# Output projection of a hybrid encoder layer: eight plain quarter products against the seven products of one Strassen step

## The chip, the cores and the metric

One core of one Trainium2 chip runs the kernel. The metric is the device time of one execution in microseconds (us). Four compute engines work side by side, each through its own queue in order: TensorE (PE: matrix products into the PSUM memory; PEld is its weight load), VectorE (DVE), ScalarE (ACT) and GpSimd (POOL). SyncE (SP) issues the DMA transfers. Instructions wait for each other through semaphores; an instruction that waits holds up all that stands behind it in its engine's queue.

## The reference, cut to what is changed

```python
y = jnp.concatenate([y_pool, y_attn], axis=-1)          # (1, 1024, 1024) f32
y = jnp.einsum('bsm,md->bsd', y, w_out[l])              # output projection, 1024 x 1024 x 1024
h = h + gate[:, None, :] * y                            # gate comes from the conditioning vector c
```

`y_pool` (512 channels) comes from pooling and a gate, `y_attn` (512 channels) from eight attention heads and a gate. Everything ahead of these lines is the same in both kernels.

## The kernel before, in words

All activations lie with channels on the 128 partitions and the 1024 positions along a row. The gated input of the projection is eight tiles of 128x1024: `yp[0..3]` (pool) and `gT[0..3]` (attention; `gT[i]` is complete when heads 2i and 2i+1 are). Precision is kept by splitting every float32 operand in two: `hi`, a copy rounded to the type that TensorE multiplies, and `lo`, the rest. A product is then three matmuls: hi by hi, hi by lo, lo by hi.

Attention is software pipelined over 64 jobs (8 heads, 8 jobs each; the loop at L1005). In one step, TensorE makes scores of one job and weighted sums of an older one (`attend`, L842), ScalarE the exponentials (L819) and their hi part (L824, `p_hi`), GpSimd the lo part (L831, `p_lo`; two of eight jobs on VectorE). When a half head is done, `out_copy` (L864) takes the sums out of PSUM: a ScalarE copy (L868) and a VectorE add (L869), both into `rb`. The next half head writes the same PSUM tile, so its `attend` waits for L869. Then VectorE takes a reciprocal (L875), GpSimd normalises (L879, `op`), TensorE turns the tile (L887, `yt`), VectorE brings it into `gT`.

`extra` (L946 and below) hangs further work into steps of that loop, by hand: `out_split` cuts two weight tiles of the projection into hi (ScalarE) and lo (GpSimd, L937), `y_split` (L900) cuts the finished tiles of y (hi on ScalarE or VectorE, L914 and L916; lo on VectorE, L918), and `fill` (L969) begins output tile 0 between the last attention matmuls.

The projection has eight output tiles. For each, `fill` issues 8 (channel tiles) x 3 (hi/lo) x 2 (halves of the positions) matmuls of 128x512 into two PSUM banks (L974, the last tile in the loop at L1110 with two of its pieces 256 wide), 384 matmuls of 512 columns by their sum. Then `out_end` (L977) adds the gated sum to x on VectorE and SP writes it out. After the attention loop GpSimd has nothing to do; VectorE makes the eight columns of the gate (`mod_col`, L108, eight instructions of 128x1024), and for each output tile one lo of 128x1024 and two final adds of 128x512.

Of the kernel before, what the change touches and what calls it, by code (L numbers as in the profile page):

```python
# [32 lines left out]
XH = 6  # L33
XS = (4, 5)
XS2 = (2, 2)
YP = ((0, 4, 5, 1), (1, 6, 7, 1), (2, 8, 8, 1), (3, 9, 9, 0), (4, 10, 10, 0), (5, 11, 11, 0), (6, 12, 12, 0))
NF = 7
SG = 12
LAG = 6
LPARTS = ((0, 512), (512, 768), (768, 1024))  # L40
# [11 lines left out]
RT = ("xh4", "xl4", "xh5", "xh1")  # L52
# [6 lines left out]
def body(ctx, tc, small, cond, xT, ada_sc, ada_sh, ada_gt, w_lat, w_fm, pool_w, w_uq, w_ukv, gains, pos, w_out, out):  # L59
# [837 lines left out]
    yh, yl = [None] * NK, [None] * NK  # L897
    yq, yk = [], []

    def y_split(k, halves=(0, 1), parts=(0, 1), he=A):  # L900
        if not yq:
            yq.append(qp.tile([P, 6, S], F32R, tag="QT", name="yq"))
            yk.append(qp.tile([P, 6, S], F32R, tag="KT", name="yk"))
        if 0 in halves and 0 in parts and k < 6:
            t_, j = (yq, yk)[k // 3][0], 2 * (k % 3)
            yh[k], yl[k] = t_[:, j], t_[:, j + 1]
        elif 0 in halves and 0 in parts:
            pool, th, tl = ((xp, "xh0", "xl0"), (dp, "t1", "t2"))[k - 6]
            yh[k] = pool.tile([P, S], F32R, tag=th, name=f"yh{k}")
            yl[k] = pool.tile([P, S], F32R, tag=tl, name=f"yl{k}")  # L910
        y = (yp + gT)[k]
        c_ = slice(halves[0] * 512, halves[-1] * 512 + 512)
        if 0 in parts and he is A:
            A.activation(yh[k][:, c_], y[:, c_], AF.Copy)  # L914
        elif 0 in parts:
            he.tensor_copy(yh[k][:, c_], y[:, c_])  # L916
        if 1 in parts:
            V.tensor_tensor(yl[k][:, c_], y[:, c_], f32(yh[k][:, c_]), ALU.subtract)  # L918

    ow = {}  # L920

    def out_load(d):
        raw = wp.tile([P, NK, P], F32, tag="raw", name=f"oraw{d}")
        SY.dma_start(raw, w_out[d])
        ow[d] = [raw]

    def out_split(d, halves=(0, 1), parts=(0, 1), eng=V):
        if 0 in halves and 0 in parts:
            for m, tag in enumerate(("whi", "wlo")):
                ow[d].append(xp.tile([P, NK, P], F32R, tag=f"x{'hl'[m]}{d + 2}", name=f"o{tag}{d}") if d < 2 else  # L930
                             wp.tile([P, NK, P], F32R, tag=tag, name=f"o{tag}{d}"))
        raw, hi, lo = ow[d]
        c_ = slice(halves[0] * 4, halves[-1] * 4 + 4)
        if 0 in parts:
            A.activation(hi[:, c_], raw[:, c_], AF.Copy)  # L935
        if 1 in parts:
            eng.tensor_tensor(lo[:, c_], raw[:, c_], f32(hi[:, c_]), ALU.subtract)  # L937
# [12 lines left out]

    at(*OL, out_load, 0)
    at(OL[0], OL[1] + 1, out_load, 1)
    for n in range(2):
        for part in range(2):
            for d in range(2):
                at(XH + d, XS[part] + XS2[d] * n, out_split, d, (n,), (part,), G)

    xr, ps = {}, {}

    def res_load(d):  # L960
        xr[d] = xp.tile([P, S], F32, tag=RT[d % 4], name=f"xres{d}")
        SY.dma_start(xr[d], xT[d])

    def new(d):
        pool, tag = (stp, "st") if d % 3 < 2 else (rsp, "r")
        t_ = pool.tile([P, 2, 512], F32, tag=tag, name=f"ops{d}")
        ps[d] = [t_[:, 0], t_[:, 1]]

    def fill(d, k0, k1, ns=(0, 1)):  # L969
        hi, lo = ow[d][1:]  # L970
        for k in range(k0, k1):
            for j, (w_, y_) in enumerate(((hi, yh), (hi, yl), (lo, yh))):
                for n in ns:
                    T.matmul(ps[d][n], w_[:, k, :], y_[k][:, n * 512:(n + 1) * 512],  # L974
                             start=(k == 0 and j == 0), stop=(k == NK - 1 and j == 2))

    def out_end(d, n):  # L977
        c_ = slice(n * 512, n * 512 + 512)
        V.scalar_tensor_tensor(xr[d][:, c_], ps[d][n], gate[:, d:d + 1], xr[d][:, c_], ALU.mult, ALU.add)
        if n:  # L980
            SY.dma_start(out[d], xr[d])
# [10 lines left out]
    at(7, 8, new, 0)  # L992
    for k in range(NF):
        at(7, 8 + k, fill, 0, k, k + 1)
    for k, s0, s1, e_ in YP:
        at(7, s0, y_split, k, (0, 1), (0,), (A, V)[e_])
        at(7, s1, y_split, k, (0, 1), (1,))
# [75 lines left out]
    fill(0, NF, 7)  # L1073
    out_tr(H - 1, (0,), avp.tile([P, 2, 512], F32, tag="av", name="ytl"))
    V.scalar_tensor_tensor(gT[3], last[0], vinv, gT[3], ALU.mult, ALU.mult)
    y_split(7)
    for d in range(2):
        res_load(d)
    out_load(2)
    for d in range(4):  # L1080
        gate_cols(d)
    new(1)
    fill(1, 0, 4)
    fill(0, 7, 8)
    for d in range(NK):
        mod_col(gate[:, d:d + 1], gc.pop(d), cb2[0])
        if d + 4 < NK:
            gate_cols(d + 4)
        if d == 3:
            out_split(2)  # L1090
    V.tensor_tensor(gate, gate, adab_s[:, 16:24], ALU.add)
    fill(1, 4, 8)
    for d in range(2, NK):
        if d + 1 < NK:
            out_load(d + 1)
# [27 lines left out]
        if d + 1 < NK:  # L1123
            out_split(d + 1)
# [69 lines left out]
```

## Time and profile before

| | us |
|---|---|
| median of three timed runs | 501.43 (501.01 to 503.52) |
| the profiled execution, its own time | 500.05 |
| span of the profiled execution | 498.3 |
| last attention sums and turned tiles on TensorE | about 409 to 416.6 |
| last matmul ends, last VectorE add ends | 494.9, 495.45 |

After the last add stand 2.85 us to the end of the span (the output transfer), and 1.75 us more to the execution's own time. Rows of the timeline read: start, duration, engine, line, operation, output<-inputs, shapes, and in brackets idle time before it with what ended that. On VectorE a row's duration runs some 0.08 us into the next row's start, so the pitch of two rows that follow each other is the time that the engine is held.

### The profile page before, as it was taken

How to read it: one execution, taken by the hardware profiler on the slowest of the kernel's cores; microseconds unless marked ns; L12 is line 12 of the kernel's file. 1: busy time of each engine (PE TensorE's matmuls, PEld its weight loads, DVE VectorE, ACT ScalarE, POOL GpSimd, SP SyncE). 2: the span in 40 equal slices, each digit the busy share in tenths (PEclk: the TensorE clock that was granted, in tenths of full speed). 3: DMA queues.
4: the chain of work that ended last, by engine and by line, in shares of the span. 5: the costliest groups of instructions: out<-in, count | busy, mean ns of one | idle time of the engine just before them, and what ended most of it. 6: DMA issues, size and time to landing. Idle time of an engine off the chain costs nothing.

```text
span 498.3 us, 7657 instructions
## 1 busy us (share of the span) xinstructions
PE 464.9 (93%) x2956; PEld 355.0 (71%) x2956; DVE 355.9 (71%) x565; ACT 253.8 (51%) x338; POOL 234.4 (47%) x190
## 2 busy tenths in 40 slices
PE   5999998999999999999989888898898969999997
PEld 3999876898888888785555555555555658888886
DVE  4888849999999853577677887877867985913221
ACT  3756038993203030226878888888899861001000
POOL 1950040201242949448869796787869780000000
PEclk9999999999999999999999999999999999999999
DMA  8894442000102110144786779779982836753333
GB/s 300 332 307 159 171 142 65 6 1 7 47 1 91 34 58 27 57 86 95 170 148 138 162 145 176 152 151 163 224 175 63 160 113 231 276 182 129 126 128 126
DMA packets 117046, 66.33 MB, mean 133 GB/s; under 512 B 105873, under 2 KB 107793, under 8 KB 117010
## 3 DMA queue, kind: packets, MB, share of 16 engines
q1 hardware_dynamic: 117010, 65.85, 49.9%
q8 instruction: 23, 0.38, 0.3%
q14 instruction: 13, 0.11, 0.1%
HBM read 35.43 MB, written 4.19 MB: 80 GB/s over the span
## 4 chain that ended last, share of the span: by engine, by line
PE 49%; DVE 22%; ACT 10%; POOL 10%; issue 5%; DMA 3%; SPq 0%; ACTq 0%; DVEq 0%; POOLq 0%
PE ops L974 14%; PE fps L170 8%; PE st L800 4%; PE pq L548 3%; ACT ph L824 3%; PE lps L234 3%; DVE bp L808 3%; POOL fraw L152 3%; ACT p L819 3%; DMA wlr<-in_w_lat 2%; PE rs L730 2%; PE av L849 2%; PE st L804 2%; POOL s L614 2%; DVE ph L831 2%
## 5 line engine op out<-in xcount | busy, mean ns | idle before, releaser
L831 POOL TENSOR_TENSOR ph<-p,ph 128x1024 f16<-128x1024 f32 x49 | 105.9, 2168 | 13.1 <-ACT ph L824 10.2
L170 PE MATMUL fps<-xh,whi 128*128 128x512 f32 x192 | 62.0, 404 | 0.5 <-ACT whi L147 0.5
L170 PE MATMUL fps<-xh,wlo 128*128 128x512 f32 x192 | 59.3, 390 | 0.1
L170 PE MATMUL fps<-xl,whi 128*128 128x512 f32 x192 | 59.3, 390 | 0.0
L800 PE MATMUL st<-q,k 97*128 97x512 f16 x192 | 49.5, 379 | 6.7 <-ACT p L819 6.6
L804 PE MATMUL st<-k,q 97*128 97x512 f16 x192 | 48.2, 379 | 8.0 <-ACT p L819 6.4
L824 ACT ACTIVATE ph<-p 128x1024 f16<-128x1024 f32 x49 | 51.7, 1055 | 0.5
L152 POOL TENSOR_TENSOR fraw<-fraw,shift 128x1024 f32<-128x1024 f32 x7 | 22.7, 3237 | 60.8 <-DVE wlo L148 53.8
L808 DVE TENSOR_REDUCE bp<-st 128x1 f32<-128x1024 f32 x32 | 39.0, 1220 | 5.2 <-PE st L804 3.4
L170 PEld LDWEIGHTS fps<-xh,whi 128*128 128x128 f32 x192 | 35.5, 189 | 9.0 <-ACT whi L147 1.0
L170 PEld LDWEIGHTS fps<-xh,wlo 128*128 128x128 f32 x192 | 36.0, 188 | 8.1 <-DVE wlo L148 0.5
L170 PEld LDWEIGHTS fps<-xl,whi 128*128 128x128 f32 x192 | 36.1, 188 | 7.7
L935 ACT ACTIVATE owhi<-oraw 128x1024 fp32r<-128x1024 f32 (+1 forms) x10 | 8.8, 885 | 54.0 <-DMA oraw<-in_w_out 54.0
L819 ACT ACTIVATE p<-st,bp,esc 128x1024 f32<-128x1024 f32 x25 | 30.1, 1204 | 9.4 <-DVE bp L809 9.0
L804 PEld LDWEIGHTS <-q 97*128 97x128 f16 x192 | 16.6, 97 | 25.6 <-issue 10.9
L800 PEld LDWEIGHTS <-k 97*128 97x128 f16 x192 | 16.6, 97 | 21.5 <-issue 8.3
L624 ACT ACTIVATE dh<-s 128x1024 fp32r<-128x1024 f32 x4 | 4.2, 1062 | 51.9 <-DVE s L621 51.9
L819 ACT ACTIVATE p<-st,ebias,esc 128x1024 f32<-128x1024 f32 x24 | 28.9, 1203 | 2.5 <-PE st L800 1.3
L850 PE MATMUL av<-VT,ph 128*128 128x65 f16 x256 | 26.4, 193 | 2.9 <-POOL ph L831 2.9
L849 PE MATMUL av<-VT,pt 128*128 128x129 f16 x256 | 28.0, 221 | 0.8 <-DMA pt<-ph 0.8
L849 PE MATMUL av<-VT,ph 128*128 128x129 f16 x256 | 27.7, 221 | 0.2 <-DVE rb L869 0.2
L850 PEld LDWEIGHTS <-ph 128*128 128x128 f16 x256 | 22.6, 98 | 7.1 <-POOL ph L831 3.1
(297 smaller groups left out, 1142.5 us busy)
## 6 DMA issues: line engine op xcount, KB each, us to landing
fraw<-in_w_fm SPq DMA_DIRECT2D x12, 512.0 KB, 3.7
asc<-in_ada_sc SPq DMA_DIRECT2D x8, 512.0 KB, 6.0
xr<-in_xT SPq DMA_DIRECT2D x8, 512.0 KB, 5.3
ash<-in_ada_sh SPq DMA_DIRECT2D x8, 512.0 KB, 6.8
oraw<-in_w_out SPq DMA_DIRECT2D x8, 512.0 KB, 5.1
xres<-in_xT SPq DMA_DIRECT2D x8, 512.0 KB, 5.0
agt<-in_ada_gt SPq DMA_DIRECT2D x8, 512.0 KB, 5.7
out_dram<-xres SPq DMA_DIRECT2D x7, 512.0 KB, 3.0
```

Of the source, the lines that this page charges most:

```text
L152: G.tensor_tensor(pb, pb, shift.unsqueeze(2).broadcast_to([P, NK, P]), ALU.mult)
L170: T.matmul(ps[n], w[:, k, :], x_[k][:, n * 512:(n + 1) * 512], start=(k == order[0] and j == 0), stop=(k == order[-1] and j == 2))
L234: T.matmul(ps[:, :LAT], l[k][:, ts_], r[k], start=(k == 0 and i == 0), stop=(k == NK - 1 and i == 2))
L800: T.matmul(stt[i][:, n], l[:HW, kt * P:(kt + 1) * P], r[:HW, 0:512], start=(a == 0), stop=(a == 2))
L804: T.matmul(stt[i][:, n], l[:HW, qt * P:(qt + 1) * P], r[:HW, n * 512:(n + 1) * 512], start=(a == 0), stop=(a == 2))
L808: V.tensor_reduce(bps[i], stt[i], AX.XY, ALU.max)
L819: A.activation(pfs[i], st, AF.Exp, bias=bps.pop(i) if hf else ebias, scale=esc)
L824: A.activation(pas[i][:, 0], pfs[i], AF.Copy)
L831: (V if in_psum(i) else G).tensor_tensor(pas[i][:, 1], pfs[i], pas[i][:, 0], ALU.subtract)
L849: T.matmul(o_, hi, VT[:, kt, h, 0:129], start=kt == 0 and qt % 2 == 0, stop=False, skip_group_check=True)
L850: T.matmul(o_[:, 0:65], lo, VT[:, kt, h, 0:65], start=False, stop=kt == NK - 1, skip_group_check=True)
L974: T.matmul(ps[d][n], w_[:, k, :], y_[k][:, n * 512:(n + 1) * 512], start=(k == 0 and j == 0), stop=(k == NK - 1 and j == 2))
```

## The change

The projection is done as one step of Strassen's algorithm in Winograd's form. Weights, y and output are cut in quarters: output tiles 0-3 and 4-7, channel tiles 0-3 (pool) and 4-7 (attention), positions 0-511 (`H0`) and 512-1023 (`H1`). Eight products of quarters become seven, each 4 output tiles x 4 channel tiles x 3 matmuls of 128x512, so 12 matmuls for one product `prod(c, d)` of one output tile, 28 such products, 336 matmuls of 512 columns in all. `a11`, `a12`, `a22` are quarters of the weights, `s1` to `s4` sums and differences of them; `b11`, `b21`, `b22` are quarters of y, `t1` to `t4` sums and differences of them. All those sums are made in float32 before the split in hi and lo.

Who does what:

- sums of y (`t1`, `t23`, `t4_split`): one VectorE instruction of 128x512 each, 16 in all, all operands in SBUF; each of the seven y operands, four channel tiles each, is then split, hi on ScalarE (`b11` and half of `t1` on VectorE), lo on VectorE;
- sums of weights (`w_comb`): VectorE, 16 in all; each of the 28 weight tiles is split, hi on ScalarE, lo on GpSimd (128x512 each);
- partial results that are used twice (`keep`): copied out of PSUM by ScalarE, 12 of 128x512, and added to x by VectorE (`pre_add`), 12 of 128x512 with both inputs in SBUF;
- the last use of a PSUM bank (`final`): VectorE adds it to x, 16 of 128x512, and SP writes 128x512 at a time.

Work moved into the attention loop: `b11` in heads 6 and 7 (VectorE, 8 instructions of 128x512), `t1` in head 7, and behind it, among the last weighted sums, `a11` and `s1` products and their weights. The gate columns (`mod_col`) stand between the splits of `t3` and `b22`.

The diff, cut to its core:

```diff
-    def fill(d, k0, k1, ns=(0, 1)):
-        hi, lo = ow[d][1:]
-        for k in range(k0, k1):
-            for j, (w_, y_) in enumerate(((hi, yh), (hi, yl), (lo, yh))):
-                for n in ns:
-                    T.matmul(ps[d][n], w_[:, k, :], y_[k][:, n * 512:(n + 1) * 512],
-                             start=(k == 0 and j == 0), stop=(k == NK - 1 and j == 2))
...
+    def t1(k, part, he=V):
+        if part == 0:
+            V.tensor_tensor(yp[k][:, H1], yp[k][:, H1], yp[k][:, H0], ALU.subtract)
+            b_hi("t1", k, yp[k][:, H1], he)
+        else:
+            b_lo("t1", k, yp[k][:, H1])
+    def t23(k):
+        V.tensor_tensor(yp[k][:, H1], gT[k][:, H1], yp[k][:, H1], ALU.subtract)
+        V.tensor_tensor(yp[k][:, H0], yp[k][:, H1], yp[k][:, H0], ALU.subtract)
+    def split(c, k, src):
+        b_hi(c, k, src)
+        b_lo(c, k, src)
+    def t4_split(k):
+        in_ring("t4", k)
+        V.tensor_tensor(yp[k][:, H1], gT[k][:, H0], yp[k][:, H1], ALU.subtract)
+        split("t4", k, yp[k][:, H1])
...
+    def w_comb(c, d, parts=(0, 1), leng=G):
...
+            if c == "s1":
+                V.tensor_tensor(src, a2[:, F_], a2[:, L_], ALU.add)
+                V.tensor_tensor(a2[:, F_], a1[:, F_], a2[:, F_], ALU.subtract)
+            elif c == "s2":
+                V.tensor_tensor(src, a2[:, L_], a2[:, F_], ALU.subtract)
+            elif c == "s4":
+                V.tensor_tensor(src, a1[:, L_], a1[:, F_], ALU.subtract)
+            A.activation(hi, src, AF.Copy)
+        if 1 in parts:
+            leng.tensor_tensor(lo, src, f32(hi), ALU.subtract)
...
+    def prod(c, d, k0=0, k1=4, cols=slice(0, 512)):
...
+        for k in range(k0, k1):
+            for j, (w_, y_) in enumerate(((hi, B[b][0]), (hi, B[b][1]), (lo, B[b][0]))):
+                T.matmul(ps[d][n][:, cols], w_[:, k], y_[k][:, cols], start=first and k == 0 and j == 0,
+                         stop=k == 3 and j == 2, skip_group_check=True)
...
+    at(7, 8, prod, "a11", 0)
+    at(7, 8, w_comb, "s1", 0)
+    at(7, 9, w_comb, "s1", 1)
+    at(7, 10, prod, "a11", 1)
...
+    y_end(H0)
+    for d in range(3):
+        keep("a11", d)
+    for k in range(4):
+        t2_split(k)
+    prod("a11", 3)
+    prod("s1", 3)
+    w_comb("s2", 0)
+    w_comb("s2", 1)
+    for d in range(2):
+        keep("s1", d)
+    keep("a11", 3)
+    for k in range(4):
+        t3_split(k)
+    keep("s1", 2)
+    keep("s1", 3)
+    w_comb("s2", 2)
+    w_comb("s2", 3)
...
+    for g, (c, d) in enumerate(seq):
+        if g + 4 < len(seq):
+            w_comb(*seq[g + 4])
+        if c == "s2":
+            prod(c, d)
+            keep(c, d)
+            b22_split(d)
+        elif c == "s3":
+            prod(c, d)
+            pre_add("s1", d)
+            final(c, d)
+            t4_split(d)
+        elif c == "s4":
+            prod(c, d)
+            pre_add("s2", d)
+            final(c, d)
+            b21_split(d)
+        elif c == "a22":
+            prod(c, d)
+            final(c, d)
+            pre_add("a11", d)
```

Removed are `y_split`, `out_split`, `fill`, `out_end` and the loop over eight output tiles.

Three places show how the queues change. First VectorE, where the sums of head 7's first half are taken out (`rb<-av71`), before and after; `yp0` to `yp2` are pool tiles, `s1` and `oraw` weights:

```order
L916 CAST yq_4188<-yp1_1225 128x1024
L875 RECIPROCAL rec60_4262<-rb_79 128x4
L918 TENSOR_TENSOR yq_4188<-yp1_1225,yq_4188 128x1024
L916 CAST yq_4188<-yp2_1226 128x1024
L918 TENSOR_TENSOR yq_4188<-yp2_1226,yq_4188 128x1024
L869 TENSOR_TENSOR rb_79<-av71_4239,rb_79 128x4x64
L831 TENSOR_TENSOR ph703_4338<-st703_4258,ph703_4338 128x1024
```

The same place in the changed kernel:

```order
L929 CAST yq_3831<-yp1_1225 128x512
L870 RECIPROCAL rec60_4271<-rb_79 128x4
L932 TENSOR_TENSOR yq6_4197<-yp1_1225,yq_3831 128x512
L947 TENSOR_TENSOR yp2_1226<-yp2_1226 128x512
L932 TENSOR_TENSOR yq7_4198<-yp2_1226,yq_3831 128x512
L1008 TENSOR_TENSOR s1_4340<-oraw4_3689 128x512
L1009 TENSOR_TENSOR oraw4_3689<-oraw0_3650,oraw4_3689 128x512
L864 TENSOR_TENSOR rb_79<-av71_4248,rb_79 128x4x64
L826 TENSOR_TENSOR ph703_4363<-st703_4267,ph703_4363 128x1024
```

Four short instructions, two of them sums of weights, now stand between the lo of `yp1` and the add into `rb`, where a cast and a lo of 1024 columns stood.

Second ScalarE at the same place (`rb<-av71` is its copy ahead of that add; `ws10` is the hi of the first `s1` weight tile):

```order
L819 ACTIVATE p702_4265<-st702_4227,ebias_72,esc_84 128x1024
L824 ACTIVATE ph701_4267<-p701_4231 128x1024
L819 ACTIVATE st703_4258<-st703_4258,ebias_72,esc_84 128x1024
L824 ACTIVATE ph702_4292<-p702_4265 128x1024
L868 ACTIVATE rb_79<-av71_4239 128x260
L824 ACTIVATE ph703_4338<-st703_4258 128x1024
```

ScalarE there in the changed kernel:

```order
L814 ACTIVATE st703_4267<-st703_4267,ebias_72,esc_84 128x1024
L819 ACTIVATE ph702_4302<-p702_4274 128x1024
L927 ACTIVATE yq_3831<-yp2_1226 128x512
L1014 ACTIVATE ws10_4339<-s1_4340 128x512
L863 ACTIVATE rb_79<-av71_4248 128x260
L819 ACTIVATE ph703_4363<-st703_4267 128x1024
```

Two hi copies, each of something that VectorE has to make first, now stand ahead of the copy out of `av71`.

Third VectorE among the products: two output tiles of the loop before, and one round of the `s3` stage now (`accv` is a kept partial result, `ops` PSUM):

```order
L937 TENSOR_TENSOR owlo4_4692<-oraw4_4638,owhi4_4691 128x1024
L979 SCALAR_TENSOR_TENSOR xres3_4640<-ops3_4642,gate_77,xres3_4640 128x512 x2
L937 TENSOR_TENSOR owlo5_4752<-oraw5_4698,owhi5_4751 128x1024
L979 SCALAR_TENSOR_TENSOR xres4_4700<-ops4_4702,gate_77,xres4_4700 128x512 x2
L937 TENSOR_TENSOR owlo6_4812<-oraw6_4758,owhi6_4811 128x1024
```

One round of the changed kernel, with one product beside it:

```order
L1013 TENSOR_TENSOR oraw0_3650<-oraw0_3650 128x512
L1055 SCALAR_TENSOR_TENSOR xres4_4647<-accv_4560,gate_77,xres4_4647 128x512
L1060 SCALAR_TENSOR_TENSOR xres4_4647<-ops0_4326,gate_77,xres4_4647 128x512
L981 TENSOR_TENSOR yp0_801<-gT0_1848,yp0_801 128x512
L932 TENSOR_TENSOR t410_4757<-yp0_801,t400_4756 128x512
```

Three VectorE instructions for 48 matmuls became five for 12, and the fifth waits for ScalarE (the hi of what the fourth makes).

More of the change, by code (lines that the diff above doesn't have):

```diff
@@ L920, in body @@
[L920 to L937, printed above, removed]
+    H0, H1 = slice(0, 512), slice(512, S)
@@ new lines, in pre_add, with final @@
+    def pre_add(c, d):
+        o, c_ = {"a11": (d, H0), "s2": (d, H1), "s1": (d + 4, H1)}[c]
+        V.scalar_tensor_tensor(xr[o][:, c_], acc[c, d], gate[:, o:o + 1], xr[o][:, c_], ALU.mult, ALU.add)
+    def final(c, d, cols=slice(0, 512)):
+        o, c0 = {"s3": (d + 4, 512), "s4": (d, 512), "a22": (d + 4, 0), "a12": (d, 0)}[c]
+        c_ = slice(c0 + cols.start, c0 + cols.stop)
+        V.scalar_tensor_tensor(xr[o][:, c_], ps[d][PRODS[c][1]][:, cols], gate[:, o:o + 1], xr[o][:, c_],
+                               ALU.mult, ALU.add)
+        SY.dma_start(out[o][:, c_], xr[o][:, c_])
@@ new lines, in body @@
+    seq = [(c, d) for c in ("s2", "s3", "s4", "a22", "a12") for d in range(4)]
+    for g, (c, d) in enumerate(seq):
+        if g + 4 < len(seq):
+            w_comb(*seq[g + 4])
+        if c == "s2":
+            prod(c, d)
[15 more added lines that the diff above has]
+            pre_add("a11", d)
+        elif d < 3:
+            prod(c, d)
+            final(c, d)
+        else:
+            for cols in (slice(0, 256), slice(256, 512)):
+                prod(c, d, 0, 4, cols)
+                final(c, d, cols)
```

217 lines of the change are left out of this document (121 added, 96 removed).

## Prediction, made before the changed kernel had run

> **What bounds the kernel now.** I read the page first: busy shares, then the forty slices.
>
> ```profile
> PE 464.9 (93%) x2956; PEld 355.0 (71%) x2956; DVE 355.9 (71%) x565; ACT 253.8 (51%) x338; POOL 234.4 (47%) x190
> PE   5999998999999999999989888898898969999997
> DVE  4888849999999853577677887877867985913221
> POOL 1950040201242949448869796787869780000000
> ```
>
> TensorE is nearly full throughout. In the last eight slices, which hold the projection, VectorE falls to two or three tenths and GpSimd to nothing. The windows of head 6, of the end of attention in two parts, and of the projection show the same in us:
>
> ```profile
> 355.70:376.30 20.60, 18.69 (x190) 11.34 (x188) 14.97 (x20) 17.74 (x20) 15.34 (x11) 1.00 0.92 189
> 391.20:409.20 18.00, 13.42 (x146) 10.00 (x144) 17.46 (x12) 15.36 (x17) 17.70 (x8) 0.99 0.36 93
> 409.20:416.60 7.40, 7.38 (x43) 6.18 (x44) 2.33 (x4) 0.39 (x1) 0.61 (x1) 0.80 1.01 397
> 416.60:495.50 78.90, 78.33 (x366) 65.26 (x365) 31.56 (x43) 7.31 (x7) 0.00 (x0) 1.00 0.46 160
> ```
>
> Columns after the length: PE, PEld, DVE, ACT, POOL busy, clock, DMA. In the projection TensorE is busy 78.3 of 78.9 us; VectorE is busy 31.6. But from 391.2 to 409.2 VectorE (17.46 of 18) and GpSimd (17.70) are both full. The chain of waits ends so:
>
> ```profile
> 416.59 67.13 PE ops L974 x294
> 483.72 5.49 PE ops L1117 x24
> 494.97 0.48 DVE xres L1119
> ```
>
> 294 matmuls in 67.13 us are 0.2283 us each, and a product of twelve is 2.74 us. Where each bank is written alone, 24 take 5.49 (0.2288): the new order of banks costs TensorE nothing.
>
> **TensorE's part.** 384 matmuls become 336: 48 x 0.2283 = 11.0 us less work. From 395.23, where the first projection matmul starts,
>
> ```profile
> 395.23 1.18 PE L974 MATMUL ops<-yq,owhi 128*128 128x512 f32 x4
> 400.11 0.22 PE L849 MATMUL av<-VT,ph 128*128 128x129 f16 x1 [0.16 <-DVE rb L869]
> 400.80 0.48 PE L974 MATMUL ops<-yq,owhi 128*128 128x512 f32 x1
> 409.22 1.12 PE L887 MATMUL yt<-ident,op 128*128 128x128 f32 x4 [0.74 <-POOL op L879]
> ```
>
> TensorE now has 28 x 2.74 = 76.7, plus 4.4 for five sets of weighted sums (0.7 each, from 400.11 to the next row shown) and two sets of turned tiles (0.45 each): without a wait it would end at 476.3, against 487.3 for 384 matmuls before, and before ended at 494.9 with 7.6 of waits. If waits stayed, 11 us would be gained. So the question is whether VectorE and GpSimd, who feed it, keep up.
>
> **What VectorE and GpSimd cost each other.** The last attention steps, VectorE first, then GpSimd:
>
> ```profile
> 391.91 3.04 DVE L918 TENSOR_TENSOR yq<-yp,yq 128x1024 fp32r<-128x1024 f32 x1
> 394.88 1.77 DVE L916 CAST yq<-yp 128x1024 fp32r<-128x1024 f32 x1
> 396.69 3.04 DVE L918 TENSOR_TENSOR yq<-yp,yq 128x1024 fp32r<-128x1024 f32 x1
> 399.65 0.41 DVE L869 TENSOR_TENSOR rb<-av,rb 128x256 f32<-128x256 f32 x1
> 399.98 1.21 DVE L831 TENSOR_TENSOR ph<-st,ph 128x1024 f16<-128x1024 f32 x1
> ```
>
> ```profile
> 379.03 1.27 POOL L937 TENSOR_TENSOR owlo<-oraw,owhi 128x512 fp32r<-128x512 f32 x1
> 391.47 2.41 POOL L831 TENSOR_TENSOR ph<-p,ph 128x1024 f16<-128x1024 f32 x1 [2.94 <-ACT ph L824]
> 393.83 2.27 POOL L937 TENSOR_TENSOR owlo<-oraw,owhi 128x512 fp32r<-128x512 f32 x1
> 396.07 2.58 POOL L831 TENSOR_TENSOR ph<-p,ph 128x1024 f16<-128x1024 f32 x1
> 398.61 1.59 POOL L879 TENSOR_TENSOR op<-rb,rec 128x256 f32<-128x256 f32 x1
> ```
>
> The times fit only if the two take turns. VectorE's lo of 391.91 gets its 1.1 us after GpSimd's ph ends at 393.88, and ends 394.95; GpSimd's owlo, issued at 393.83, then needs its 1.2 and ends 396.10; the cast ends 396.65, the next ph 398.65, the next lo 399.73, op 400.20. Not one of them overlaps another. VectorE's L831, which reads one operand from PSUM, runs its usual 1.21 beside GpSimd. So a VectorE instruction with all operands in SBUF and a GpSimd instruction take the time of both. The change puts some 80 such VectorE instructions and 26 weight lo of GpSimd into the last 110 us.
>
> **The VectorE queue, added up.** Durations:
>
> ```profile
> 126.43 0.68 DVE L645 TENSOR_TENSOR KT<-KT,rqk 128x512 f32<-128x512 f32 x1
> 127.03 0.42 DVE L647 TENSOR_TENSOR KT<-krr,rqk 128x256 f32<-128x256 f32 x1
> 422.05 1.22 DVE L108 SCALAR_TENSOR_TENSOR agt<-agt,cb 128x1024 f32<-128x1024 f32 x1
> 423.20 1.23 DVE L108 SCALAR_TENSOR_TENSOR agt<-agt,cb 128x1024 f32<-128x1024 f32 x1
> L979 DVE SCALAR_TENSOR_TENSOR xres<-ops,gate,xres 128x512 f32<-128x512 f32 x14 | 9.9, 746 | 10.2 <-PE ops L974 10.1
> L935 ACT ACTIVATE owhi<-oraw 128x512 fp32r<-128x512 f32 x4 | 2.5, 626 | 0.0
> 389.12 0.69 DVE L916 CAST yq<-yp 128x1024 fp32r<-128x1024 f32 x1
> ```
>
> A 128x512 sum or lo holds VectorE 0.60 (126.43 to 127.03), a gate column 1.15, a final add 0.67 (0.746 less the 0.08 that rows overlap), a `pre_add` 0.63 (not in the trace; between those two), a half cast 0.33. A hi on ScalarE is 0.63, and a VectorE instruction that waits for it stands 0.77 with the hand-overs. One turn of GpSimd is 1.23 (a weight lo), 2.1 (ph) or 0.6 (op). I walked the new queues row by row, giving each side its turn as above, from 389.12, where `t1` takes the place of the first cast:
>
> - to the add into `rb`: 8 sums and lo x 0.60, 2 casts, 2 small ones = 5.9; turns of ph713, ph700, op, ph701, ph702 that fall on VectorE = 8.1; ScalarE waits 1.2. It is reached at 404.4; before, at 399.65. ScalarE's copy ahead of it stands behind the hi of `s1`, which needs the sixth of those sums. TensorE has the `a11` product as cover to 398.7, then waits 6.1 us. (Such a wait also costs clock: after TensorE's wait up to 409.22 the window of 7.4 us shows 0.80, 1.5 us lost. Here it would be lost ahead of the next wait, for the last turned tile, which is longer.)
> - to the first gate column: 30 x 0.60 = 18.1, other 3.2, seven turns 6.7, waits for ScalarE and TensorE 4.2 (of which 2.8 for the hi of `t3`, behind TensorE's last `a11`): 404.4 + 32.2 = 436.6. TensorE waits 2.0 for the last turned tile, 1.5 and 1.9 for `s2` weights meanwhile.
> - gate columns and `b22`: 8 x 1.15 + 4 x 0.60 + 0.1 = 11.7; six turns, for the weights of the end of `s2` and of `s3`, 7.4: 455.7. TensorE has worked through `s3` at 455.5 and now waits for `s4`: its first sum is still to be made.
> - four rounds of `s3` on VectorE: sum, pre_add, final, sum, lo = 3.1; the wait for ScalarE's hi before the lo 0.77; a turn of 0.70 (GpSimd begins under the final add, whose PSUM operand lets both run): 4.6 each against 2.74 for a product: 455.7 + 18.3 = 474.0. TensorE loses 2.9 before `s4`, 1.85 in each later round.
> - four rounds of `s4`: pre_add, final, lo = 1.9, and two turns, 1.8, since GpSimd works off the weights of `a22` and `a12` without a pause: 14.8, so 488.8. The last lo of `b21` is needed by the first `a12`; TensorE, done with `a22` at 486.3, waits 2.6.
> - then four products, 11.0, the last drain 0.2 and the last half add 0.5: 500.5.
>
> The chain is VectorE's from 389 to 489; before, the last add ended at 495.45. So the sum is +5.1, not -11: TensorE's 11 us go, but its waits rise from 7.6 to 23.
>
> Costs at nothing: ScalarE's 12 `keep` and the hi copies (it was busy 7.3 of 78.9 us; a 512-column copy lies under a 2.74 product, and without that cover is 0.6 each); output in eight more, smaller transfers, of which only the last ends the span, as before. Heads 6 and 7 take eight more VectorE instructions for `b11`, 3.7 us of work; GpSimd is busy 15.34 of 20.6 us in head 6, so each waits some 0.74 x 1.05 (half a ph) more, 6 in all. VectorE idles 5.6 us a head, 27%. A gain is excluded, since nothing leaves VectorE there, and the weight lo that leave GpSimd are in the walk. Ends: 0, if the idle time takes it, and +6, if the 6 of waits end up in the exponentials' way; I take +2, nearer to the idle time.
>
> One row differs from turns. GpSimd was kept out for long here, VectorE's next row that reads PSUM being 167.54:
>
> ```profile
> 159.40 9.98 POOL L152 TENSOR_TENSOR fraw<-fraw,shift 128x1024 f32<-128x1024 f32 x1 [8.97 <-DVE wlo L148]
> 167.54 1.28 DVE L527 TENSOR_TENSOR u<-fps,rb 128x512 f32<-128x512 f32 x2
> ```
>
> A run of short VectorE instructions held it off for 8 us. The Trainium skill, "SBUF — State Buffer", section "Who interferes with whom", says that a VectorE instruction with two SBUF inputs and a GpSimd one that reads SBUF exclude each other, and the second fully blocks until the first finishes. By that rule GpSimd waits for one instruction and the sum is the one above; the rows at 391 to 400 agree (0 us overlap), the row at 159.40 does not.
>
> **Rivals.**
>
> - *VectorE keeps GpSimd out* (as at 159.40) through the eight gate columns. Then GpSimd makes the weights of the third `s2` product only after them: TensorE stands 10 us there, from 436.1 to 446.1, and has 18 products left, 49.3, with 1.4 of waits: last add 497.5, so +2.1. For it: that row. Against: the rows at 391 to 400, and later gate columns wait for their transfers, which lets GpSimd in:
>
> ```profile
> 428.30 1.23 DVE L108 SCALAR_TENSOR_TENSOR agt<-agt,cb 128x1024 f32<-128x1024 f32 x1 [0.33 <-DMA agt<-in_ada_gt]
> ```
>
> Chance 0.17.
> - *Faster: turns cost VectorE little*, because GpSimd's short lo fits into VectorE's own waits and final adds, or ScalarE and VectorE hand over faster than 0.77. All turns in the five parts are 8.1 + 6.7 + 7.4 + 2.8 + 7.2 = 32.2; without any, VectorE would be done before TensorE, which then ends at 477 and, with the waits that stay, 481. With half of them, VectorE's chain ends at 484.4. For it: VectorE's own work is only some 59 of these 100 us. Against: no overlap in the rows. 481 to 494 for the last add; likeliest 487. Chance 0.27.
> - *Slower still: `b11` in heads 6 and 7* delays the row maxima, for which ScalarE's exponentials wait, by the full 6 us, so 512.5 in the end. For it: VectorE and GpSimd are both three quarters busy there. Against: a quarter is idle. Chance 0.12.
>
> That TensorE does not save the 48 matmuls I rule out; its instructions are counted.
>
> **The numbers.** The profiled execution took 500.05 for a last add at 495.45, so 4.6 are added; the median of the runs is 501.43, 1.4 more. Forecast: 500.5 + 2 + 4.6 + 1.4 = 508.5, with chance 0.44; own range 503 to 512. With the same 8 added to each last add, VectorE keeping GpSimd out gives 505.5, the faster rival 489 to 502, at 495; `b11` gives 512.5. The range holds the walk with its errors and most of the faster rival: 491 to 513. About 0.5% (2.5 us) is what a measurement of this kernel can tell. Faster: 0.24 (most of its rival). Slower: nearly all of the forecast, `b11` and most of VectorE keeping GpSimd out, 0.62. Within: 0.14.
>
> **What would show it.** Right: in the changed profile no GpSimd weight lo overlaps a VectorE SBUF instruction; TensorE waits about 6 us for `rb` near 399 to 405; it waits before `s4` and in its rounds; VectorE is above eight tenths up to 489. Wrong: VectorE idle and TensorE without waits after 430 (then the faster rival), a wait of 10 us at the third `s2` product (GpSimd kept out), or the first weighted sums of the `rb` wait's job reached several us after 398.7 (`b11`).

## The result, and the profile of the changed kernel

| kernel | median, us | kernel before, same chip | ratio (95% interval) |
|---|---|---|---|
| changed kernel | 509.17 (508.54 to 509.64, 4 runs) | 501.22 (4 runs) | 1.0154 (1.0113 to 1.0196) |

The change makes the kernel 1.5% slower: 509.17 us, where 508.5 was forecast. The profiled execution took 508.54, its span is 506.8, its last VectorE add ends at 504.05 (before: 495.45).

The page of the changed kernel, busy shares and slices:

```profile
PE 459.1 (91%) x2896; PEld 346.4 (68%) x2896; DVE 405.8 (80%) x627; ACT 275.2 (54%) x385; POOL 274.3 (54%) x214
PE   5999998999999999999988888988897698895796
DVE  4888849999999672757678778787998989798892
POOL 1940040201433949447969779796877862572550
```

The picture of before is turned round at the right end. VectorE's last slices, two or three tenths before, read seven to nine almost to the end; GpSimd works on into the last tenth of the span; TensorE falls to five, six and seven in places. The stretch from the first `t1` sum (before: the cast at its place) to the last add shows it in numbers (columns after the length: PE, PEld, DVE, ACT, POOL busy, clock, DMA). Before:

```profile
389.12:495.45 106.33, 100.94 (x562) 82.18 (x559) 53.43 (x62) 25.14 (x27) 18.31 (x9) 0.98 0.49 163
```

The changed kernel, the stretch and four parts of it:

```profile
391.27:504.05 112.78, 94.02 (x502) 73.07 (x499) 95.71 (x116) 46.66 (x75) 56.30 (x33) 0.95 0.42 147
399.00:417.00 18.00, 12.46 (x100) 10.08 (x99) 14.87 (x15) 9.84 (x14) 12.21 (x8) 0.81 0.55 204
437.00:457.20 20.20, 18.89 (x84) 15.21 (x82) 20.17 (x25) 8.35 (x16) 13.30 (x6) 1.00 0.69 251
457.20:475.70 18.50, 11.66 (x48) 8.11 (x47) 15.28 (x21) 5.69 (x10) 5.13 (x5) 1.00 0.32 124
475.70:489.30 13.60, 11.39 (x43) 8.65 (x42) 13.18 (x14) 5.83 (x11) 13.12 (x8) 0.87 0.15 58
```

VectorE is full with the gate columns (20.17 of 20.2 us from 437.0), and in the rounds of `s3` (from 457.2) TensorE works 11.66 of 18.5 us. This is where TensorE's 11.0 us went. Its idle time in the stretch rose from 106.33 - 100.94 = 5.4 to 112.78 - 94.02 = 18.8 us, by 13.4. Its busy time fell by 6.9 only: it ran at 0.95 of its clock, not at 0.98, and a product that starts behind a wait takes 3.0 us (at 459.57) and not 2.74. Together +6.5. The other 2.15 of the 8.6 us by which the last add is later had been lost ahead of the stretch (it begins at 391.27, not 389.12), 0.45 of them in the first 270 us, where both kernels do the same.

The chain of waits of the last part, from the profile's chain with a window, leaves TensorE for VectorE behind the row of 441.32, that is at 454.8, and comes back at 488.7:

```profile
441.32 13.47 PE ops L1033 x58
455.40 1.89 DVE yq L932 x3
457.89 0.67 DVE xres L1055
458.67 0.75 DVE xres L1060
459.42 1.10 DVE yp L981
...
475.79 1.72 DVE xres L1055
...
488.67 12.61 PE ops L1033 x60
```

### The profile page after: what moved, and what is told of

Same layout as the page of the kernel before. It is cut to its first block, busy times and chain, and to the rows that moved or that the text cites. A ratio compares the mean times of both kernels' runs of the same rounds, so it can differ in the third digit from the quotient of the medians.

```text
span 506.8 us, 7740 instructions
## 1 busy us (share of the span) xinstructions
PE 459.1 (91%) x2896; PEld 346.4 (68%) x2896; DVE 405.8 (80%) x627; ACT 275.2 (54%) x385; POOL 274.3 (54%) x214
## 4 chain that ended last, share of the span: by engine, by line
PE 40%; DVE 29%; POOL 12%; ACT 9%; issue 7%; DMA 3%; SPq 0%; ACTq 0%; DVEq 0%; POOLq 0%
PE ops L1033 9%; PE fps L165 8%; PE st L795 4%; POOL ph L826 4%; PE pq L543 3%; POOL fraw L147 3%; PE av L844 2%; PE st L799 2%; DMA wlr<-in_w_lat 2%; PE rs L725 2%; ACT ph L819 2%; ACT p L814 2%; PE lps L229 2%; POOL s L609 2%; PE pk L553 2%
## 5 line engine op out<-in xcount | busy, mean ns | idle before, releaser
L826 POOL TENSOR_TENSOR ph<-p,ph 128x1024 f16<-128x1024 f32 x49 | 106.2, 2174 | 12.5 <-ACT ph L819 9.8
L1033 PE MATMUL ops<-yq,ws 128*128 128x512 f32 x144 | 34.9, 395 | 6.8 <-DVE xres L1060 6.8
L1033 PEld LDWEIGHTS ops<-yq,ws 128*128 128x128 f32 x144 | 26.3, 188 | 14.2 <-ACT ws L1014 8.4
L799 PEld LDWEIGHTS <-q 97*128 97x128 f16 x192 | 16.6, 97 | 25.6 <-issue 10.9
```

Of the source, the lines that this page charges most:

```text
L799: T.matmul(stt[i][:, n], l[:HW, qt * P:(qt + 1) * P], r[:HW, n * 512:(n + 1) * 512], start=(a == 0), stop=(a == 2))
L826: (V if in_psum(i) else G).tensor_tensor(pas[i][:, 1], pfs[i], pas[i][:, 0], ALU.subtract)
L1033: T.matmul(ps[d][n][:, cols], w_[:, k], y_[k][:, cols], start=first and k == 0 and j == 0, stop=k == 3 and j == 2, skip_group_check=True)
```

## The experiments

Each kernel is the changed kernel with one edit. The differences "to the changed kernel" are differences of the ratios to the kernel before on the same chip, times 501 us. The half widths of the two intervals, 2.1 us for the changed kernel and about 1.2 for a run, make some 2.4 us for a difference: what is smaller cannot be told from nothing by the times, and for it the text reads the trace, from an event ahead of the edit. That is one trace of each kernel.

| kernel | median, us | ratio (95% interval) | to the changed kernel |
|---|---|---|---|
| no_pool_lo (work left out) | 499.75 | 0.9988 (0.9971 to 1.0005) | -8.3 |
| rb_first | 506.28 | 1.0120 (1.0099 to 1.0140) | -1.7 |
| lo_on_vector | 506.60 | 1.0124 (1.0106 to 1.0142) | -1.5 |
| late_adds | 501.97 | 1.0031 (1.0016 to 1.0045) | -6.2 |
| early_gate | 509.38 | 1.0165 (1.0138 to 1.0192) | +0.6 |
| early_gate_b | 508.19 | 1.0151 (1.0126 to 1.0176) | -0.2 |
| t4_ahead | 506.39 | 1.0101 (1.0077 to 1.0124) | -2.7 |
| no_b11 (work left out) | 508.57 | 1.0147 (1.0122 to 1.0173) | -0.4 |
| all_moves | 499.49 | 0.9967 (0.9947 to 0.9987) | -9.4 |
| three_moves | 500.25 | 0.9971 (0.9953 to 0.9989) | -9.2 |
| four_moves_b | 498.41 | 0.9958 (0.9937 to 0.9980) | -9.8 |
| three_moves_lov | 498.14 | 0.9937 (0.9910 to 0.9964) | -10.9 |

### Do VectorE and GpSimd take turns, and does it cost the end? (no_pool_lo)

```diff
-        if 1 in parts:
+        if c in ("s2", "s3", "s4", "a22", "a12"):
+            W[c, d] = (hi, hi)
+        elif 1 in parts:
             leng.tensor_tensor(lo, src, f32(hi), ALU.subtract)
```

> The 20 weight lo of s2, s3, s4, a22 and a12 are left out on GpSimd; their matmuls read the hi again, so TensorE, VectorE, ScalarE and the transfers have the same work. Theory (VectorE and GpSimd take turns, and VectorE's queue sets the end): six of the eight gate columns fall from 2.25 us apart to 1.15 (6.7 us less), the first add of each s4 round from 1.79 to 0.74 and the sums of the s3 rounds from 1.18 to 0.68, so VectorE gets through its queue some 12 us earlier and the last add comes near 492 instead of 504. Rival 1 (the gate columns are slow because eight 512 KB transfers and eight more for x land at that time): they stay 2.25 apart and the end moves by 2 us at most. Rival 2 (TensorE's own waits set the end): its one wait for a weight lo, 1.3 us, goes, and no more.

First the timeline of the changed kernel, VectorE's gate columns (L103) and GpSimd's weight lo (L1016) beside them:

```profile
438.92 1.22 DVE L103 SCALAR_TENSOR_TENSOR agt<-agt,cb 128x1024 f32<-128x1024 f32 x1
440.06 2.28 DVE L103 SCALAR_TENSOR_TENSOR agt<-agt,cb 128x1024 f32<-128x1024 f32 x1
...
453.46 1.22 DVE L103 SCALAR_TENSOR_TENSOR agt<-agt,cb 128x1024 f32<-128x1024 f32 x1
```

```profile
439.14 4.36 POOL L1016 TENSOR_TENSOR ws<-oraws,ws 128x512 fp32r<-128x512 f32 x2 [3.83 <-ACT ws L1014]
443.46 2.29 POOL L1016 TENSOR_TENSOR ws<-oraw,ws 128x512 fp32r<-128x512 f32 x1
```

The first column, which GpSimd's first lo has to let pass, and the last, with no GpSimd work beside it, take 1.22; the six between take 2.3, and GpSimd's lo, 1.27 elsewhere, take 2.2 each. Each waits for one instruction of the other. Now the run without these lo:

```profile
438.98 1.22 DVE L103 SCALAR_TENSOR_TENSOR agt<-agt,cb 128x1024 f32<-128x1024 f32 x1
440.12 1.22 DVE L103 SCALAR_TENSOR_TENSOR agt<-agt,cb 128x1024 f32<-128x1024 f32 x1
...
445.95 1.23 DVE L103 SCALAR_TENSOR_TENSOR agt<-agt,cb 128x1024 f32<-128x1024 f32 x1 [1.13 <-DMA agt<-in_ada_gt]
```

All columns take 1.22, with the same transfers in flight, so the first rival falls. VectorE's `b21` work ends 11 us earlier (478.3, not 489.3). The end comes 8.3 us earlier in the times, 9.0 in the trace (last add 495.0), not 12: the columns now overtake their transfers (1.1 + 0.5 + 0.6 us of waits), and from 471.5 on TensorE is the bound, with eight products of 2.74 still to make. The second rival (1.3 us) falls as well.

### TensorE's longest wait (rb_first)

```diff
-    at(7, 8, w_comb, "s1", 0)
+    at(7, 9, w_comb, "s1", 0)
     at(7, 9, w_comb, "s1", 1)
```

> The two sums and the split of the first s1 weight tile are moved from ahead of the copy and add out of the sums of head 7's first half to behind them; nothing is left out. Theory (VectorE's queue sets the end): TensorE's wait of 5.3 us for that add falls to 1 to 2, and its clock does not drop to 0.5 there (another 1.3), but VectorE has the same instructions to do and gains only the 0.9 and 0.3 that it stands for ScalarE there: the end comes 1 us earlier, 1.5 at most. Rival (TensorE's waits add up to the end): 5 to 6.5 us earlier.

TensorE's wait for the add into `rb` fell from 5.3 to 1.7 us. Counted from the add into `rb` of head 6's first half (380.77 in the changed kernel, 380.19 here), the add waited for came 3.7 us earlier, the first gate column 2.3, the last add 2.3. So neither number held: 3.6 of TensorE's wait bought 2.3 at the end (its wait for the last turned tile grew from 0.3 to 1.6), and VectorE, which has the same instructions, gained 2.3, not 1. The timeline shows why; the changed kernel, VectorE and GpSimd:

```profile
400.73 1.61 DVE L932 TENSOR_TENSOR yq<-yp,yq 128x512 fp32r<-128x512 f32 x1 [0.93 <-ACT yq L927]
402.26 2.60 DVE L1008 TENSOR_TENSOR s<-oraw 128x512 f32<-128x512 f32 x1
...
405.91 0.42 DVE L864 TENSOR_TENSOR rb<-av,rb 128x256 f32<-128x256 f32 x1 [0.32 <-ACT rb L863]
```

```profile
399.21 5.11 POOL L826 TENSOR_TENSOR ph<-p,ph 128x1024 f16<-128x1024 f32 x2
```

And VectorE in rb_first, where GpSimd's same two instructions end at 403.73:

```profile
401.66 0.41 DVE L864 TENSOR_TENSOR rb<-av,rb 128x256 f32<-128x256 f32 x1
401.99 1.21 DVE L826 TENSOR_TENSOR ph<-st,ph 128x1024 f16<-128x1024 f32 x1
...
405.58 0.69 DVE L1008 TENSOR_TENSOR s<-oraw 128x512 f32<-128x512 f32 x1
```

In the changed kernel the weight sum L1008, all SBUF, stands 1.9 us beside GpSimd's second `ph`. In rb_first the add into `rb` and L826, which each read one operand from PSUM, run at full speed there, and the sum comes when GpSimd is done. The order of VectorE's instructions decides how many turns it pays for. The clock expectation failed too: behind the shorter wait the granted clock still fell, to 0.57 from 403 to 407.

### More work for VectorE (lo_on_vector)

The edit gives the lo of the last two `s2` and all `s3` weights to VectorE and spreads the gate columns between them:

```diff
+    w_comb("s2", 2, (0,))
+    w_comb("s2", 3, (0,))
...
+    gcol(0)
+    w_comb("s2", 2, (1,), V)
+    w_comb("s2", 3, (1,), V)
+    for d in range(4):
+        w_comb("s3", d, (0,))
+        prod("s2", d)
+        keep("s2", d)
+        gcol(2 * d + 1)
+        w_comb("s3", d, (1,), V)
+        if d < 3:
+            gcol(2 * d + 2)
```

> Six weight lo (the last two of s2, all of s3), which GpSimd makes beside the gate columns, are made by VectorE between the gate columns; GpSimd stands idle there; nothing is left out. Theory (turns): VectorE has 6 x 0.60 = 3.6 us more to do and is held up 6.7 us less, so it reaches the s4 sums 3.1 us earlier and the end is 2.5 to 3 us earlier: an engine that gets more work is done sooner. Rival (the gate columns are slow for another reason, such as transfers): 3.6 us later.

```profile
440.88 1.29 DVE L1016 TENSOR_TENSOR ws<-oraws,ws 128x512 fp32r<-128x512 f32 x2
442.09 1.22 DVE L103 SCALAR_TENSOR_TENSOR agt<-agt,cb 128x1024 f32<-128x1024 f32 x1
...
452.24 1.23 DVE L103 SCALAR_TENSOR_TENSOR agt<-agt,cb 128x1024 f32<-128x1024 f32 x1 [1.38 <-DMA agt<-in_ada_gt]
```

VectorE needs 16.74 us from the first column to the first `s4` sum (439.74 to 456.48), not 18.29 (438.92 to 457.21): 1.55 less with six instructions more. Of the expected 3.1, 1.4 went into the wait for the last column's transfer. The rival, 3.6 more, falls. The last add comes 1.25 earlier, counted from the first column; the times say -1.5, which alone would be inside the intervals.

### VectorE's rounds (late_adds, t4_ahead)

late_adds takes the adds of kept results out of the rounds and puts them, with their output, into the last two stages:

```diff
-        SY.dma_start(out[o][:, c_], xr[o][:, c_])
+        if c not in ("s3", "s4"):
+            SY.dma_start(out[o][:, c_], xr[o][:, c_])
...
         elif c == "s3":
             prod(c, d)
-            pre_add("s1", d)
             final(c, d)
...
             prod(c, d)
-            pre_add("s2", d)
             final(c, d)
...
             final(c, d)
             pre_add("a11", d)
+            late_add("s1", d)
         elif d < 3:
             prod(c, d)
+            late_add("s2", d)
+            if d == 2:
+                late_add("s2", 3)
             final(c, d)
```

> The eight adds of kept partial results that stand ahead of the final adds of s3 and s4 are moved behind those, into the a22 and a12 stages, where VectorE waits for TensorE; the output of these halves goes out after them; nothing is left out. Theory (VectorE's queue sets when a22 starts): an s3 round falls from 4.62 to about 4.0 us, an s4 round from 3.39 to what TensorE needs, a22 starts some 4 to 5 us earlier (near 474 instead of 478.5) and so does the end. Rival (TensorE's own work and its waits elsewhere set the end): no change, within 1 us.

One round of the `s3` stage on VectorE, the changed kernel, then late_adds:

```profile
457.21 0.68 DVE L1013 TENSOR_TENSOR oraw<-oraw 128x512 f32<-128x512 f32 x1
457.81 0.74 DVE L1055 SCALAR_TENSOR_TENSOR xres<-accv,gate,xres 128x512 f32<-128x512 f32 x1
458.67 0.75 DVE L1060 SCALAR_TENSOR_TENSOR xres<-ops,gate,xres 128x512 f32<-128x512 f32 x1
459.34 1.18 DVE L981 TENSOR_TENSOR yp<-gT,yp 128x512 f32<-128x512 f32 x1
461.21 0.69 DVE L932 TENSOR_TENSOR t<-yp,t 128x512 fp32r<-128x512 f32 x1 [0.70 <-ACT t L927]
461.82 0.68 DVE L1013 TENSOR_TENSOR oraws<-oraws 128x512 f32<-128x512 f32 x1
```

```profile
457.80 0.68 DVE L1013 TENSOR_TENSOR oraw<-oraw 128x512 f32<-128x512 f32 x1
458.40 0.74 DVE L1065 SCALAR_TENSOR_TENSOR xres<-ops,gate,xres 128x512 f32<-128x512 f32 x1
459.06 0.68 DVE L981 TENSOR_TENSOR yp<-gT,yp 128x512 f32<-128x512 f32 x1
460.44 0.98 DVE L932 TENSOR_TENSOR t<-yp,t 128x512 fp32r<-128x512 f32 x1 [0.70 <-ACT t L927]
461.35 0.68 DVE L1013 TENSOR_TENSOR oraws<-oraws 128x512 f32<-128x512 f32 x1
```

A round falls from 4.61 to 3.55. From the first gate column, `a22` starts 34.5 us on (439.52 to 474.00), not 39.6 (438.92 to 478.49): 5.1 earlier, and the end comes 6.2 earlier in the times, 7.2 in the trace: the four `a22` products take 10.9 us here and 13.0 in the changed kernel, where they wait for `s4`'s final adds (see the tail, below). VectorE's instructions are the same; only their place changed, into stages where it would stand idle, and with it the time of eight outputs. The rival (no change) falls.

t4_ahead makes the lo of a `t4` tile one round after its sum:

```diff
-            t4_split(d)
+            t4_sum(d)
+            if d:
+                b_lo("t4", d - 1, yp[d - 1][:, H1])
+            if d == 3:
+                b_lo("t4", 3, yp[3][:, H1])
```

> In the rounds of s3 the lo of a t4 tile is made one round after its sum, so that VectorE does not stand for ScalarE's hi; nothing is left out. Theory (VectorE's queue sets when a22 starts, and each of these waits of 0.70 us counts in full): three of the four waits go, the rounds fall from 4.62 to 3.9 us, the end comes 2 us earlier. Rival (the wait of VectorE is where GpSimd has its turn, so that the turn moves to another place): 0.5 us or less.

The four rounds took 15.55 us (458.85 to 474.40), not 18.49 (457.21 to 475.70), 2.9 less, and the end came 2.7 earlier in the times, 3.0 in the trace, counted from the first gate column. That is more than the 2 expected, since the fourth wait went too: the last two lo stand together and the hi of the second is done by then. Here VectorE's wait had not been GpSimd's turn.

### A wait that was cover (early_gate, early_gate_b)

Both put all `s2` sums and some gate columns ahead of the lo of `t3`, for which VectorE had stood 2.74 us. They differ in ScalarE's order and in how many columns come first, four in early_gate, two in early_gate_b. early_gate:

```diff
+    for d in range(4):
+        w_comb("s2", d)
+    keep("a11", 3)
...
+    for k in range(4):
+        b_hi("t3", k, yp[k][:, H0])
+    for d in range(4):
         keep("s1", d)
...
     for d in range(NK):
+        if d == 4:
+            for k in range(4):
+                b_lo("t3", k, yp[k][:, H0])
```

early_gate_b:

```diff
     for d in range(2):
         keep("s1", d)
     keep("a11", 3)
...
+    for d in range(2, 4):
+        w_comb("s2", d)
     keep("s1", 2)
     keep("s1", 3)
...
+    for k in range(4):
+        b_hi("t3", k, yp[k][:, H0])
     for d in range(NK):
+        if d == 2:
+            for k in range(4):
+                b_lo("t3", k, yp[k][:, H0])
```

> All four sums of s2, then four of the eight gate columns, are put ahead of the four lo of t3, for which VectorE stood 2.7 us waiting for ScalarE; ScalarE's copies are ordered to match; nothing is left out. Theory (VectorE's queue sets the end): VectorE reaches the s4 sums 2.7 us earlier, near 454.5 instead of 457.2, TensorE's wait of 1.3 us for the third s2 weight goes, and the end comes 2.5 to 3 us earlier. Rival (it is TensorE's waits that count): 1.3 us earlier.

> As early_gate, but the copies of the s1 results stand ahead of the hi of t3 on ScalarE, as in the changed kernel, and the lo of t3 follow the second gate column. In early_gate TensorE got a new wait of 3.6 us for one of these copies, and the lo of t3 and the gate columns took 2.5 us more of GpSimd's turns. If the copies were why early_gate gained nothing, the end now comes 2.5 us earlier than in the changed kernel. If it was the turns (VectorE's idle 2.7 us had been where GpSimd made two weight lo undisturbed), VectorE reaches the s4 sums at most 0.8 us earlier than in the changed kernel, and the end comes 0 to 1 us earlier.

Neither gained. In early_gate TensorE got a wait of its own:

```profile
438.65 1.78 PE L1033 MATMUL ops<-t,ws 128*128 128x512 f32 x5 [3.58 <-ACT accv L1050]
```

By the kernel's code the first `s2` product writes one bank of a PSUM tile of two, and the copy that it waited for reads the other (`keep` of `s1`, now behind the hi of `t3`). In early_gate_b that wait is gone, and the time is still that of the changed kernel. From the start of the last `a11` product to the last piece it takes 73.0 us (431.12 to 504.12), early_gate also 73.0 (429.34 to 502.37), the changed kernel 73.6 (428.21 to 501.85): 0.6 where 2.5 was to be gained, and `s4`'s first sum comes 0.6 earlier too. This is what was expected if it was the turns. GpSimd's two lo that had run in VectorE's idle time in the changed kernel,

```profile
432.76 1.29 POOL L1016 TENSOR_TENSOR ws<-oraw,ws 128x512 fp32r<-128x512 f32 x1 [6.48 <-ACT ws L1014]
434.00 1.30 POOL L1016 TENSOR_TENSOR ws<-oraws,ws 128x512 fp32r<-128x512 f32 x1
```

now fall on VectorE's work: in early_gate_b the four lo of `t3` take 6.61 us, not 2.50. That is 4.1 more; as four gate columns are slow and not six, 2.2 of it had been paid there before, and the other 1.9 are what the 2.74 us of idle time had covered.

```profile
440.21 6.61 DVE L932 TENSOR_TENSOR yq<-yp,yq 128x512 fp32r<-128x512 f32 x4 [0.19 <-ACT yq L927]
```

### The term for heads 6 and 7 (no_b11)

The edit takes `b11` out of heads 6 and 7 and lets the `a11` products read something else:

```diff
+        if b == "b11":
+            B[b] = ([hi.rearrange("p k c -> p (k c)")] * 4,) * 2
...
-    for k in range(4):
-        at(6 + (2 + 2 * k) // 8, (2 + 2 * k) % 8, b11, k, 0)
-        at(6 + (3 + 2 * k) // 8, (3 + 2 * k) % 8, b11, k, 1)
```

> The eight VectorE instructions that split b11 in heads 6 and 7 are left out; the a11 products read their own weight hi as the moving operand instead. This prices a term of the sum: +2 for b11 in heads 6 and 7. If it holds, the last exponentials of head 7 and all behind them come 1.5 to 2 us earlier and so does the end; if VectorE's idle time takes b11, 0; by the rival of full turns, 6.

The times show 0.4, not distinguishable from 0. In the trace, counted in each kernel from the same add in head 3 (326.38 before, 326.85, 327.61 here), the last exponential starts 69.58 us on before, 71.18 in the changed kernel and 70.36 here: `b11` cost 0.8 of the 1.6. The stretch repeats well: in ten of the twelve runs that keep `b11` it is 71.15 to 71.20, but in t4_ahead and early_gate_b 72.8, and of the kernel before there is one trace. The other 0.8 is there without `b11`; where it comes from stays open.

### The edits together

These have no edit of their own: all_moves is rb_first, late_adds, t4_ahead and early_gate; three_moves leaves early_gate out; four_moves_b puts early_gate_b in its place, three_moves_lov lo_on_vector.

> Four changes of order together: the first s1 tile behind the add out of the sums, the adds of kept results late, the gate columns in the ScalarE wait, the lo of t4 one round late; nothing is left out. Theory: VectorE's queue is then 12 to 14 us shorter up to the start of a22, so that TensorE becomes the bound: from its next-to-last wait, near 425, it has 22 products of 2.74 us, 60.4, so the last add is near 487 to 490 and the time 493 to 497, 1 to 1.5% below the kernel before. Rival (turns go to other places, and VectorE stays the bound): 499 to 502.

> rb_first, late_adds and t4_ahead together, without early_gate. If each took time from VectorE's queue alone and it stays the bound up to s4, their gains add: 2.2 + 6.5 + 2.4 = 11.1 us less than the changed kernel, 497 to 498. From s4 on TensorE is the bound: 12 products of 2.74 us, 32.9, behind a start near 456, so the last add near 490.

> three_moves and early_gate_b together. If TensorE's 3.6 us wait for a ScalarE copy was what held all_moves, that wait goes and TensorE runs 22 products of 2.74 us from 425.7 with 1 to 2 us of waits: last add near 488, time 494 to 495. If VectorE with its turns is still the bound up to s4, the time is that of three_moves within 1 us.

> three_moves and lo_on_vector together. Theory (turns): VectorE reaches s4 1.5 us earlier than in three_moves, and TensorE's waits before the third s2 weight and before s4 shrink by 0.5 and 1.5: 1.5 to 2 us less than three_moves. Rival (VectorE's 3.6 us more of work count): 1 to 3 us more than three_moves.

all_moves (with early_gate) kept the 3.6 us wait above and took 499.49, not the 493 to 497 expected: what its rival said (499 to 502). three_moves gave -9.2 of the 10.6 that its three parts gave alone. four_moves_b lies 0.6 below three_moves; its 498.41 are not the 494 to 495 expected of a TensorE almost without waits, which in its trace still waits 3.1 us for GpSimd's lo at `s2` and `s4`. three_moves_lov has the lowest ratio, 0.6% (0.4 to 0.9) below the kernel before, and its order is the one that the theory gives: VectorE makes six lo more. It lies 1.7 us below three_moves, where 1.5 to 2 were expected; the intervals of these four kernels overlap, so which of them is fastest is not shown. Its TensorE waits from 425 on:

```profile
PE ops L1038 <- POOL ws L1021: 1.9, 2, 1.5
PE ops L1038 <- DVE ylast L890: 1.2, 1, 1.2
PE ops L1038 <- DVE xres L1070: 1.0, 2, 0.6
PE ops L1038 <- DVE ws L1021: 0.8, 1, 0.8
```

4.9 us, where the changed kernel has 12.1 from the same wait for `ylast` on (9.6 for `xres`, 1.3 for a weight lo, 1.2 for `ylast`).

## Why the prediction held, point by point

Waypoints of the walk, moved by 2.15 us, the time by which the changed kernel reached its start later:

| point | walk + 2.15 | measured |
|---|---|---|
| add into `rb`, head 7's first half | 406.6 | 405.9 |
| first gate column | 438.8 | 438.9 |
| first `s4` sum | 457.9 | 457.2 |
| rounds of `s3` done | 476.2 | 475.7 |
| last lo of `b21` | 491.0 | 489.3 |
| last add ends | 502.7 | 504.05 |

- **Turns.** Right: columns of 2.3 beside lo of 2.2, 1.22 when GpSimd's lo are taken away. The Trainium skill, "SBUF — State Buffer", section "Who interferes with whom", says that of two such instructions the second fully blocks; these rows agree (a column of 1.15 and a lo of 1.1 make 2.25). The rival that VectorE keeps GpSimd out through the eight columns fell: GpSimd had every second turn. Why it was held off for 8 us at 159.40 stays open.
- **VectorE's queue as the bound to 489.** Right, up to the last final add of `s4` (488.5); late_adds and t4_ahead, which change VectorE's order and leave it the same instructions, moved the end by 6.2 and 2.7.
- **The wait for `rb`.** 6.1 forecast, 5.3 measured. That it lies ahead of a longer bound was right (3.6 us of it bought 2.3); what VectorE gains there when the order is changed was not seen: PSUM-reading instructions take no turn.
- **The rounds.** 4.6 forecast, 4.62 measured for `s3`; 3.7 and 3.40 for `s4`.
- **The tail.** The step that failed: the walk let TensorE run through `a22` without a wait, to be done at 486.3 + 2.15, and wait 2.6 us for the last lo of `b21`. That lo was ready at 489.3, 1.7 earlier than the walk has it, and TensorE was late instead. Each `a22` product goes into the PSUM tile whose other bank the final add of `s4` with the same number reads, and waits for that add; these adds come one `s4` round apart. The start of `a22` in the changed kernel (up to 481), and its second product in rb_first:

```profile
478.49 2.95 PE L1033 MATMUL ops<-t,wa 128*128 128x512 f32 x7 [2.05 <-DVE xres L1060]
```

```profile
478.96 3.00 PE L1033 MATMUL ops<-t,wa 128*128 128x512 f32 x12 [0.39 <-DVE xres L1060]
```

  In the changed kernel the clock was low here too:

```profile
478.00:482.00 4.00, 3.51 (x9) 2.81 (x10) 3.90 (x5) 2.26 (x5) 4.00 (x4) 0.61 0.17 66
```

  But this did not set the end. In rb_first the clock stayed at 1.00 (475 to 488.6) and the four `a22` products took 13.0 us all the same, with waits of 0.4 for the final adds; in both kernels the last of them starts behind the last final add of `s4` (488.67 in the changed kernel). From the end of the last final add of `s4` to the end of the last add it takes 15.5 us in the changed kernel (488.53 to 504.05), in rb_first, lo_on_vector, t4_ahead, early_gate and early_gate_b: behind VectorE's last round five products are left, not the four of the walk. So 11.7 were forecast from the last lo of `b21` on, and 14.75 measured: 2.2 until `a22` is done, 0.6 for a wait of the last product's second half for the final add of its first (501.31), which the walk does not have, and 0.2 more. The two errors, 1.65 early and 3.05 late, leave 1.4. Behind the last add 4.6 + 1.4 were added; measured 4.5 (504.05 to 508.54) and 0.6 (to the median). So that 508.5 comes so near to 509.17 is in part luck: 1.4 too little and 0.9 too much nearly cancel.
- **Heads 6 and 7.** +2 forecast, 1.6 measured, but by no_b11 only half of it is `b11`. The term had the size and, for half of it, not the cause.
- **TensorE's 11 us.** 23 of waits were forecast, and 18.8 of idle time measured from 391.27 on. The forecast's waits are all that lies between the work at full speed and its end; counted so, 25.1 were measured (the last matmul ends at 503.54, less 2.15 and 476.3). What the walk left out is the slower running: as an estimate from the two windows, 3.5 us more of reduced clock than before (0.05 of 112.78 against 0.02 of 106.33 us). Part of it lay under waits for VectorE, as in `a22`, and cost nothing.

## What to carry to other kernels

Before an algorithm that trades matmuls for sums, add up the queue of the engine that makes the sums, stage by stage, and count for every instruction with all operands in SBUF the turn of GpSimd that falls on it; a helper on GpSimd can cost VectorE more (1.1 us for one lo) than the work itself (0.6). Put what can be late (adds of kept results) where that engine idles anyway, and put instructions that read PSUM beside GpSimd's long ones. An idle stretch of VectorE may be cover for GpSimd: filling it gained 0.6 us here, where 2.5 was expected. And ask for every product which instruction last reads the PSUM tile that it writes into: in `a22` that was a final add at the end of VectorE's queue.

## What the runs showed of the hardware that was not expected

- The granted clock fell behind some waits and not behind others of the same length. Behind a 1.6 us wait for the last turned tile, four transposes and a 1.2 us wait for `ylast`, the next product took 3.0 us in rb_first, all_moves and four_moves_b, but 4.5 in three_moves and 5.5 in three_moves_lov, with a window at 0.50 (in the changed kernel, where the first of the two waits is 0.3, 3.0 at 428.21):

```profile
425.00:431.00 6.00, 5.64 (x13) 4.46 (x14) 4.67 (x8) 1.80 (x4) 1.09 (x1) 0.50 0.01 3
```

  Behind the wait of 2.05 us before `a22` the clock fell to 0.61 in the changed kernel (the window from 478 shown above); behind 2.02 us in rb_first it stayed at 1.00. The Trainium skill, "TensorE: Matmul & The Clock Gate", section "Part 1: The HAM clock gate (the "warmup" mystery)", says that the gate watches a free-running window, so that the same kernel's slow stretch varies from run to run; that fits, and no run here tests it. A product of 4.5 or 5.5 us in place of 3.0 is as much as the smaller effects above, so these were read from the trace between two events, not from one time.
- A VectorE cast with a single SBUF input takes turns too, as the prediction reads the one at 394.88 in the kernel before (1.77 us, where the one at 389.12 takes 0.69):

```profile
393.99 2.24 DVE L929 CAST yq<-yp 128x512 fp32r<-128x512 f32 x1
```

  2.24 us beside GpSimd's `ph`, where the cast before it (391.99) took 0.43.
